# Masks, PSUM banks, the end of the experts and the rows handed to the mixers

## The chip, the cores and the metric

The kernel runs on one core of a Trainium2 chip. The metric is the device time of one execution in microseconds (us); a comparison takes the median of several runs. Engines are named as the profile names them: PE (TensorE, matmuls), PEld (its weight loads), DVE (VectorE), ACT (ScalarE), POOL (GpSimd) and SP (SyncE, which issues most DMAs). Each engine works through its own queue in order.

## The reference

Three blocks follow one another on 256 tokens of width 1024, in float32:

```python
def reference(x, c, ...):
    x = first_block(...)    # Fourier and conv branches, then a mixture of 16 experts, final norm
    x = second_block(...)   # "hybrid": compressed and windowed attention, block attention, gated merge, w_o
    return third_block(...) # two layers of four token mixers and a feed-forward, final norm

# first_block, experts: each expert takes its 32 best tokens
a = einsum('becd,edf->becf', xe, w_gate_e); u = einsum('becd,edf->becf', xe, w_up_e)
y = einsum('becf,efd->becd', silu(a) * u, w_down_e)
y = y * vals[..., None]                       # then added back at the tokens' rows
x = x + gate_f[:, None, :] * moe_out; return rms_norm(x, g_final)
# second_block, end
return x + rms_norm_2(m @ w_o, norm_post)
# third_block, one layer
h = rms_norm_3(x, attn_norm[l]); proj = h @ w_in[l]
o_a = neighborhood_attention(qa, ka, va, na_rpb[l])   # bias by offset, masked to 8 x 16 neighbours
o_b = diff_attention(qb, kb, vb, lam, ..., t5_diff)   # bias table t5, heads 0 to 3
o_c = dilated_attention(qc, kc, vc, t5_dil)           # bias table t5, heads 4 to 7, three windows merged
o_d = mla_attention(q_nope, q_rope, k_nope, k_rope, v_d)
x = x + concat([o_a, o_b, o_c, o_d]) @ w_o[l]
x = x + (silu(h2 @ w_gate[l]) * (h2 @ w_up[l])) @ w_down[l]
```

The dilated attention merges three windows; the kernel does it with one softmax whose scores get the t5 bias and a mask `c_dil`, the logarithm of how many of the windows hold the offset (and -1e30 where none does). Its value depends on the offset of key and query alone.

## The kernel before

**Storage and products.** Tokens lie in two halves (h = 0, 1) of 128 partitions, `x` is 128 x 2 x 1024. A projection needs the input transposed (features on partitions, tiles k = 0 to 7 of 128 features). To get float32 accuracy every operand is split into two fp32r parts, high and low (`hi`, `lo`; `wh`, `wl`): ACT casts the high part (L125 for weights, L284 for inputs), DVE subtracts for the low part (L126, L285), and PE makes three matmuls (L173, L174, L175) for each k and half. `proj` (L149) takes two PSUM banks, one for each half, and works through the weights in the order of their loads: k by k, for both halves. With `ahead=3` the last three pieces are split first and then run half by half, so that half 0 is evacuated while half 1 computes. Weights come through six ring slots, loaded by SP in an order fixed by `load` (L75).

**PSUM.** There are eight banks: pool `mm` has five (projections, attention scores, expert accumulators), `tr` two (transposes, L271), and `po` one. In `po` lie the up product of an expert (`psU`), the attention outputs (`po`), the output of the differential heads (`od`, L1603), one accumulator of `shift_scale`, the Fourier output and the router's `pb`.

**Queues.** The program is written in one order, and a scheduler of the framework orders the instructions of each engine by when they are ready in its model. Side work (generators, stepped by `pump` after each product piece) puts attention between projections. `tc.issue_after(ins)` keeps an instruction behind another. `N.held` (L130) keeps the next splits of weights behind an instruction.

**End of the experts** (L780 to L910). The last expert runs its down projection in two halves of 512 columns, each: 16 float32 matmuls L901 into `py` (the profile counts two records for each, so 32), `Y` = `py` times gate (L903, DVE), two matmuls that scatter `Y` to the tokens (`acc`, L907, four records), then `out(n)` (L813): two adds to `x`, transposes (L271) with their splits, squares, gain. Meanwhile the first weights of the hybrid block are loaded into ring slots and split there (`next_load`), and their products with the first input half's tiles k = 0 to 3 (`next_products`, 24 matmuls) are put into the second half after the fourth of its 16 matmuls; tiles 4 to 7 come at the end.

**Hybrid block to mixers** (L1245 to L1293). `w_o_2` runs in two chunks of 512 columns; the evacuation of the last (L1280 to L1287) makes the norm and adds `mo` times `r` to `x`, half by half in four steps of 256 columns. Then `nxt.half(c)` transposes four feature tiles of both halves at once, 128 x 256 for a split. The mixers' first projection, 416 columns (`chunk(2304, 416, ...)`, L1491), reads that input from the tile `hx`, which until then held the operand `mh`, `ml` of `w_o_2`.

**Mixers** (L1319 on, once in each of two layers). The projections run with four attention groups beside them: MLA first (its softmax reads the scores straight from the bank: L1395, ACT L1404), then differential, neighbourhood and dilated heads. `bias_rows` (L1296) in block 1 computes the t5 table for all offsets into DRAM (`t5d`); `na_bias` loads a 128 x 2048 tile and adds a mask to it on POOL (L1366); `dil_bias` loads the t5 tile, loads `c_dil` into an `m2` slot (L1372), and adds it on POOL in four adds (L1374). `m2` is a pool of scratch tiles: four in block 1, eight in the mixers.

## Time and profile before

| what | us |
|---|---|
| median of 3 runs | 2061.4 (2057.15 to 2067.67) |
| profiled execution | 2060.89 |
| its span, first to last instruction | 2059.1 |
| PE busy | 1658.0 (81%) |
| DVE busy | 810.1 (39%) |
| ACT busy | 602.7 (29%) |
| POOL busy | 171.9 (8%) |
| chain that ended last | PE 47%, DMA 43%, DVE 6%, issue 2% |

The span has stages: block 1 to about 252 us, the experts to about 1154, their end to 1190, the hybrid block to 1395, the way into the mixers to 1430, mixers and feed-forward of layer 0 to 1745, and of layer 1 to the end. A row of a timeline gives start, duration, engine, line, operation, output <- input, the count, and in brackets how long the engine was idle before it and what released it. A window gives each engine's busy time and instruction count, the mean granted clock of PE (1.00 is 2.4 GHz, 0.50 is 1.2 GHz), the busy share of the DMA engines and their GB/s.

### The profile page before, as it was taken

The numbers are of one execution on the slowest core, as the hardware profiler recorded it, in microseconds if no ns is written. First come the engines' busy times: TensorE is split into PE (matmuls) and PEld (weight loads), VectorE is DVE, ScalarE is ACT, GpSimd is POOL, SyncE is SP. The second block draws the span as 40 slices with busy tenths as digits, with TensorE's granted clock in tenths as the row PEclk, the third lists the DMA queues.
The fourth block names the chain that finished last, engine by engine and source line by source line (L and its number), as shares of the span: only waits on it lengthen the run. The fifth ranks groups of instructions, "written<-read, shape, count | busy, mean of one in ns | idle before, by whom it ended". The sixth has DMA issues, their size and how long they took to land.

```text
span 2059.1 us, 22375 instructions
## 1 busy us (share of the span) xinstructions
PE 1658.0 (81%) x8897; PEld 997.9 (48%) x8897; DVE 810.1 (39%) x1565; ACT 602.7 (29%) x1075; POOL 171.9 (8%) x135
## 2 busy tenths in 40 slices
PE   7999796665655565656555799999999999999998
PEld 4777631111111111111111387777768888768886
DVE  4788610000000000000000357786885555785554
ACT  4455410000000000000000245555554445555443
POOL 1652100000000000000000131102000000110000
PEclk9999898768788888887887999999999999999999
DMA  9988789999999999999999873446335556525552
GB/s 361 378 297 340 319 363 429 429 428 429 430 428 430 429 428 431 429 430 429 429 428 430 332 257 127 143 136 221 117 103 184 184 172 218 170 68 184 184 174 72
DMA packets 128441, 616.24 MB, mean 299 GB/s; under 512 B 8264, under 2 KB 17672, under 8 KB 101328
## 3 DMA queue, kind: packets, MB, share of 16 engines
q1 hardware_dynamic: 124336, 601.46, 74.1%
q0 software_dynamic: 3568, 12.75, 1.9%
q8 instruction: 70, 1.15, 0.2%
q10 hardware_dynamic: 432, 0.60, 0.1%
q14 instruction: 35, 0.29, 0.0%
HBM read 613.72 MB, written 4.24 MB: 300 GB/s over the span
## 4 chain that ended last, share of the span: by engine, by line
PE 47%; DMA 43%; DVE 6%; issue 2%; ACT 1%; SPq 1%; POOL 0%; POOLq 0%; ACTq 0%; DVEq 0%
DMA wr<-we_gate_dram 13%; DMA wr<-we_up_dram 13%; DMA wr<-we_down_dram 13%; PE pb L173 13%; PE pb L174 12%; PE pb L175 12%; DMA wr<-w_in_dram 2%; DVE wl L126 2%; PE pb L271 1%; DMA wr<-w_ada_dram 1%; PE pb L851 1%; PE pb L1413 1%; PE pb L901 1%; ACT sb L1404 1%; PE pb L793 1%
## 5 line engine op out<-in xcount | busy, mean ns | idle before, releaser
L126 DVE TENSOR_TENSOR wl<-wr,wh 128x1024 fp32r<-128x1024 f32 (+1 forms) x380 | 410.2, 1088 | 263.5 <-ACT wh L125 260.0
L851 PE MATMUL pb<-wr,XT 128*32 128x512 f32 x2048 | 319.4, 753 | 214.7 <-DMA wr<-we_up_dram 121.6
L125 ACT CAST wh<-wr 128x1024 fp32r<-128x1024 f32 (+1 forms) x380 | 339.9, 898 | 329.8 <-PE pb L175 302.3
L173 PE MATMUL pb<-wh,hx 128*128 128x512 f32 (+3 forms) x992 | 388.5, 392 | 3.4 <-ACT sb L1404 2.0
L174 PE MATMUL pb<-wl,hx 128*128 128x512 f32 (+3 forms) x992 | 376.6, 380 | 1.7 <-DVE wl L126 1.6
L175 PE MATMUL pb<-wh,hx 128*128 128x512 f32 (+3 forms) x992 | 377.2, 381 | 0.0
L851 PEld LDWEIGHTS pb<-wr,XT 128*32 128x32 f32 x2048 | 61.3, 124 | 454.5 <-DMA wr<-we_up_dram 198.4
L901 PE MATMUL pb<-wr,hT 128*32 128x512 f32 x1024 | 172.7, 803 | 103.0 <-DMA wr<-we_down_dram 96.4
L868 DVE TENSOR_TENSOR hs<-pb,hs 128x512 f32<-128x512 f32 x16 | 11.1, 691 | 554.9 <-PE pb L851 554.9
L173 PEld LDWEIGHTS pb<-wh,hx 128*128 128x128 f32 x992 | 187.2, 189 | 44.0 <-issue 5.8
L174 PEld LDWEIGHTS pb<-wl,hx 128*128 128x128 f32 x992 | 187.7, 189 | 36.5 <-DVE wl L126 4.5
L175 PEld LDWEIGHTS pb<-wh,hx 128*128 128x128 f32 x992 | 187.4, 189 | 35.4 <-issue 0.7
L867 ACT ACTIVATE hs<-pb 128x512 f32<-128x512 f32 x16 | 9.6, 598 | 535.3 <-PE pb L851 534.2
L901 PEld LDWEIGHTS pb<-wr,hT 128*32 128x32 f32 x1024 | 33.9, 129 | 221.0 <-DMA wr<-we_down_dram 143.2
L903 DVE TENSOR_TENSOR Y<-pb,gfr 128x512 f32<-128x512 f32 x15 | 10.4, 692 | 247.1 <-PE pb L901 247.1
L881 ACT COPY Sc<-pb 128x256 f32<-128x256 f32 x16 | 6.0, 373 | 310.3 <-PE pb L879 310.3
L821 POOL TENSOR_TENSOR x<-x,grow 128x512 f32<-128x512 f32 x4 | 5.6, 1420 | 890.5 <-ACT jk L260 890.5
L173 PE MATMUL pb<-wh,ah 128*128 128x512 f32 x176 | 69.9, 397 | 0.0
L174 PE MATMUL pb<-wl,ah 128*128 128x512 f32 x176 | 69.6, 395 | 0.0
L175 PE MATMUL pb<-wh,al 128*128 128x512 f32 x176 | 69.6, 395 | 0.0
L907 PE MATMUL acc<-Y,Sc 64*128 64x512 f32 (+1 forms) x128 | 40.7, 714 | 18.3 <-DVE Y L903 18.3
L404 POOL TENSOR_SCALAR wr<-wr,cs 128x768 f32<-128x768 f32 x14 | 40.3, 2878 | 31.3 <-DMA wr<-w_ada_dram 26.4
(504 smaller groups left out, 1727.4 us busy)
## 6 DMA issues: line engine op xcount, KB each, us to landing
wr<-we_gate_dram SPq DMA_DIRECT2D x64, 2048.0 KB, 38.9
wr<-we_up_dram SPq DMA_DIRECT2D x64, 2048.0 KB, 39.0
wr<-we_down_dram SPq DMA_DIRECT2D x63, 2048.0 KB, 38.9
wr<-w_in_dram SPq DMA_DIRECT2D x62, 1024.0 KB, 8.0
wr<-w_ada_dram SPq DMA_DIRECT2D x24, 1024.0 KB, 12.7
wr<-w_gate_dram SPq DMA_DIRECT2D x22, 1024.0 KB, 5.1
wr<-w_up_dram SPq DMA_DIRECT2D x22, 1024.0 KB, 5.0
wr<-w_down_dram SPq DMA_DIRECT2D x20, 1024.0 KB, 5.0
```

The lines of the kernel that those rows point to most:

```text
L125: self.nc.scalar.copy(hi, src)
L126: self.nc.vector.tensor_tensor(lo, src, hi.bitcast(F32), ALU.subtract)
L173: nc.tensor.matmul(o, xh[:, kt, tok], hv[:, k, :], start=kt == first, stop=False)
L174: nc.tensor.matmul(o, xh[:, kt, tok], lv[:, k, :], start=False, stop=False)
L175: self.last_mm = nc.tensor.matmul(o, xl[:, kt, tok], hv[:, k, :], start=False, stop=kt == last).ins
L271: self.nc.tensor.transpose(pv[:, j, h * P:(h + 1) * P], src[:, h, (k + j) * P:(k + j + 1) * P], self.ident)
L404: nc.gpsimd.tensor_scalar(wp, wp, cs[:, k:k + 1], None, ALU.mult)
L793: nc.tensor.matmul(pg, part[:, h, k * P:(k + 1) * P], G[:, h, es].rearrange("p e c -> p (e c)"), start=(h == 0 and i == 0), stop=(h == 1 a ...
L851: N.last_mm = nc.tensor.matmul(pacc[32 * j:32 * j + 32, :], XT[:, k + kk, e, :], wt[:, kk, j * 512:(j + 1) * 512], start=(k + kk == 0), st ...
L901: nc.tensor.matmul(py[32 * q:32 * q + 32, :], hT[:, b, 32 * j:32 * j + 32], wt[:, i, n * 512 - c0:n * 512 - c0 + 512], start=first, stop=l ...
L907: nc.tensor.matmul(acc[n][h], Sc[r, h * P:(h + 1) * P], Y[r, :], start=(e == 0), stop=(e == NE - 1))
L1404: nc.scalar.activation(sb[:, c], (ps if bias is None else sb)[:, c], AF.Exp, bias=mm[:, h:h + 1], accum_out=sm[:, h:h + 1])
```

## The change

The edits, in the order of the file:

- **PSUM.** The pool `po` is gone and `mm` has six banks; all that lay in `po` comes from `mm`.
- **A head in proj.** `lead=n` splits the first n pieces, then runs their products for half 0 and after that for half 1. The mixers' first projection of layer 0 uses `lead=3`.
- **Rows by halves.** `InputT.rows(h)` transposes one token half: two banks of four 128 x 128 transposes, each tile split by itself. The hybrid block queues `rows(0)` right behind half 0's adds and calls `rows(1)` at the end, then the squares. `mh`, `ml` move from `hx` to two tiles of the pool `ap82`. `N.held` keeps one split behind the second step of half 0's adds, where before three stood behind that of half 1.
- **End of the experts.** `out` issues the next load, and its splits only behind the second add of `x`. The second half's matmuls L901 and the products are chained in written order: eight of the sixteen L901 (`at + i`), the products of tiles 0 and 1, the other eight, tile 2 behind `Y`, tile 3 behind the adds, tiles 4 to 7 at the end.
- **Masks.** `c_dil` becomes an 8 x 512 table over heads and offsets (zero for heads 0 to 3). `bias_rows` loads it into the tile `t5sb` and adds the product to it, where before it copied the product; `dil_bias` with its load and four adds is gone. The mask of `na_bias` is added in eight operations of 128 x 256, where before it was one of 128 x 2048.

```diff
-        self.mm, self.tr, self.po = ps("mm", 5), ps("tr", 2), ps("po", 1)
+        self.mm, self.tr = ps("mm", 6), ps("tr", 2)
...
+        if lead:
+            head = [(k, piece, self.split_w(piece)) for k, piece in islice(pieces, lead)]
+            for h in range(2):
+                for k, piece, hl in head:
+                    self.proj_piece(ps, xh, xl, k, piece, n, hl=hl, hs=(h,))
...
+    def rows(self, h):
+        N, nc, tok = self.N, self.N.nc, slice(h * P, (h + 1) * P)
+        for k in range(0, KT, 4):
+            pv = N.bank(N.tr).rearrange("p (k t) -> p k t", t=P)
+            for j in range(4):
+                nc.tensor.transpose(pv[:, j, :], N.x[:, h, (k + j) * P:(k + j + 1) * P], N.ident)
+            for j in range(4):
+                g = self.gain[:, k + j:k + j + 1]
+                nc.scalar.activation(self.hi[:, k + j, tok], pv[:, j, :], AF.Copy, scale=g)
+                nc.vector.scalar_tensor_tensor(self.lo[:, k + j, tok], pv[:, j, :], g, self.hi[:, k + j, tok].bitcast(F32),
+                                               ALU.mult, ALU.subtract)
...
-            if n:
-                with tc.issue_after(add):
-                    next_load()
+            ahead = next_load()
+            next(ahead)
+            with tc.issue_after(add):
+                next(ahead, None)
+            if n:
+                next_products(1)
...
-                        if c0 and at + i == 4:
-                            next_products()
+                        if c0 and at + i == 8:
+                            next_products(2)
...
+                            with N.queued() if c0 else nullcontext():
+                                mm = nc.tensor.matmul(py[32 * q:32 * q + 32, :], ...
+                            if c0:
+                                N.last_mm = mm.ins
                 nc.vector.tensor_tensor(Y, py, ...)
+                if c0:
+                    next_products(1)
...
-                    self.po = N.po.tile([P, 512], F32, tag="b", name="po")
+                    self.po = N.bank(N.mm, "po")
...
-        mh, ml = N.hT()
+        mh, ml = N.T("mh"), N.T("ml")
...
-                        if q == 256 and h == 1:
-                            N.behind(st.ins)
+                        if q == 256 and h == 0:
+                            N.held = [st.ins]
+                    if h == 0:
+                        N.soon(lambda: nxt.rows(0))
...
+        nxt.rows(1)
         for c in range(2):
-            nxt.half(c)
+            nxt.squares(c)
...
-    nc.vector.tensor_copy(sb, pb[:8, :])
+    nc.gpsimd.dma_start(sb, a["c_dil"])
+    nc.vector.tensor_tensor(sb, pb[:8, :], sb, ALU.add)
...
-            nv = nb.rearrange("p h n (r c) -> p (h n r) c", c=64)
-            nc.gpsimd.tensor_tensor(nv, nv, nmask.unsqueeze(1).to_broadcast([P, 32, 64]), ALU.add)
+            for h in range(2):
+                for n in range(4):
+                    nv = nb[:, h, n, :].rearrange("p (r c) -> p r c", c=64)
+                    nc.gpsimd.tensor_tensor(nv, nv, nmask.unsqueeze(1).to_broadcast([P, 4, 64]), ALU.add)
...
-        def dil_bias():
-            td = t5_bias(4, "t5b")
-            dm = N.m2.tile([P, 2, S], F32, tag="m2", name="dm")
-            nc.gpsimd.dma_start(dm, a["c_dil"].rearrange("p (h k) -> p h k", h=2))
-            for n in range(4):
-                nc.gpsimd.tensor_tensor(td[:, n], td[:, n], dm, ALU.add)
-            return td
...
-        chunk(2304, 416, [(crow, f1)])
+        chunk(2304, 416, [(crow, f1)], lead=0 if l else 3)
...
-                    od.append(N.bank(N.po))
+                    od.append(N.bank(N.mm))
```

## Rows read from the trace of the kernel before

**Rows 1.** Windows of the span by stage; the first line names the columns

```profile
core 0: us, PE busy (x) PEld busy (x) DVE busy (x) ACT busy (x) POOL busy (x), PEclk, DMA share, GB/s
252.00:1154.00 902.00, 552.36 (x3328) 130.59 (x3328) 52.13 (x102) 21.74 (x43) 3.18 (x3) 0.81 0.99 423
1154.00:1190.00 36.00, 29.40 (x149) 19.18 (x150) 20.47 (x38) 17.46 (x36) 11.71 (x16) 0.95 0.79 289
1395.00:1430.00 35.00, 31.54 (x142) 25.48 (x141) 25.59 (x68) 22.43 (x47) 6.30 (x10) 0.95 0.67 217
1430.00:1535.00 105.00, 100.02 (x546) 75.82 (x545) 80.45 (x230) 53.56 (x130) 15.30 (x12) 0.98 0.37 118
1760.00:1860.00 100.00, 93.32 (x516) 70.19 (x515) 79.56 (x219) 50.26 (x125) 11.29 (x8) 1.00 0.36 115
```

**Rows 2.** Timeline of DVE, end of the experts: start, duration, instruction, [idle before <- releaser]

```profile
1155.46 1.23 DVE L126 TENSOR_TENSOR wr<-wr 128x1024 fp32r<-128x1024 f32 x1 [9.53 <-ACT wr L125]
```

**Rows 3.** Timeline of PE, end of the experts

```profile
1157.43 3.45 PE L907 MATMUL acc<-Y,Sc 128*128 128x512 f32 x4 [3.96 <-DVE Y L903]
...
1162.48 1.06 PE L901 MATMUL pb<-wr,hT 128*32 128x512 f32 x8
...
1169.14 2.78 PE L901 MATMUL pb<-wr,hT 128*32 128x512 f32 x24
1172.74 1.98 PE L907 MATMUL acc<-Y,Sc 128*128 128x512 f32 x4 [0.81 <-DVE Y L903]
```

**Rows 4.** Issues of the last three loads of down weights: count, first and last start, landing

```profile
L75 SPq DMA_DIRECT2D wr<-we_down_dram x3: 4185/4212/4763, 1125.4 to 1133.9; - x3
...
DMA to landing us min/median/max: 30.0/31.9/33.7
```

**Rows 5.** Timeline of DVE, hybrid block to mixers

```profile
1395.01 1.67 DVE L1287 SCALAR_TENSOR_TENSOR x<-mo,ro_r,x 128x256 f32<-128x256 f32 x4 [0.70 <-POOL ro_r L241]
...
1399.07 1.67 DVE L1287 SCALAR_TENSOR_TENSOR x<-mo,ro_r,x 128x256 f32<-128x256 f32 x4 [0.67 <-POOL ro_r L241]
```

**Rows 6.** Timeline of PE, hybrid block to mixers

```profile
1396.24 0.39 PE L175 MATMUL pb<-wh,hx 128*128 128x512 f32 x1
...
1399.61 1.54 PE L271 MATMUL pb<-ident,x 128*128 128x128 f32 x6 [2.76 <-DVE x L1287]
```

**Rows 7.** Windows behind that wait and in the first mixers (columns as in rows 1)

```profile
1399.30:1402.40 3.10, 2.74 (x9) 2.30 (x10) 3.10 (x8) 2.27 (x7) 0.62 (x1) 0.51 0.00 0
1450.60:1454.00 3.40, 3.40 (x13) 2.93 (x12) 2.63 (x5) 1.23 (x2) 0.00 (x0) 0.50 0.00 0
```

**Rows 8.** Timeline of PE, mixers of both layers, its waits

```profile
1449.69 0.70 PE L1413 MATMUL pb<-qkT 96*128 96x256 f32 x2 [1.88 <-ACT sb L1404]
...
1772.60 0.50 PE L173 MATMUL pb<-wh,hx 128*128 128x512 f32 x1 [2.02 <-ACT sb L1404]
...
1776.38 0.70 PE L1413 MATMUL pb<-qkT 96*128 96x256 f32 x2 [1.66 <-ACT sb L1404]
```

**Rows 9.** Timeline of DVE, mixers of both layers, beside the mask's add

```profile
1441.61 2.78 DVE L126 TENSOR_TENSOR wl<-wr,wh 128x1024 fp32r<-128x1024 f32 x1
...
1766.23 5.12 DVE L126 TENSOR_TENSOR wl<-wr,wh 128x1024 fp32r<-128x1024 f32 x1
```

**Rows 10.** One line each: counts, least, median, longest ns, first and last start

```profile
L1366 POOL TENSOR_TENSOR nb<-nb,nmask x2: 4585/4711/4837, 1438.5 to 1765.7; 128x2048 f32<-128x2048 f32 x2
...
L1374 POOL TENSOR_TENSOR t5b<-t5b,dm x8: 1262/1296/1320, 1490.6 to 1819.4; 128x512 f32<-128x512 f32 x8
...
L1420 DVE TENSOR_SCALAR sb<-sb,cs x64: 338/349/1355, 1445.8 to 1849.7; 128x256 f32<-128x256 f32 x64
```

**Rows 11.** Waits of SP's queue, 118 to 140 us

```profile
SPq L75 <- DVE modT L390: 12.1, 1, 12.1
```

**Rows 12.** Window of block 1 (columns as in rows 1)

```profile
138.00:169.10 31.10, 31.10 (x137) 25.44 (x137) 25.00 (x29) 16.46 (x27) 18.22 (x8) 0.97 0.86 319
```

**Rows 13.** Timeline of POOL, block 1

```profile
192.05 0.59 POOL L1310 DMA_DIRECT2D t5v<-t5sb  x1 [23.00 <-DVE t5sb L1309]
```

More of the change, by code (lines that the diff above doesn't have):

```diff
@@ L2 @@
 from contextlib import ExitStack, contextmanager, nullcontext
+from itertools import islice
 import numpy as np
@@ L147, in split_w, with proj @@
         return hv, lv
-    def proj(self, xh, xl, loads, n, evac, ahead=0):
+    def proj(self, xh, xl, loads, n, evac, ahead=0, lead=0):
         ps = [self.bank(self.mm), self.bank(self.mm)]
@@ L1448, in st3 @@
                     return
-                po = N.po.tile([P, 512], F32, tag="b", name="po")
+                po = N.bank(N.mm, "po")
                 pts = [pTs.pop(n - 1), pTs.pop(n)]
@@ L1785, in consts @@
     c["c_t5oh"] = (np.arange(32)[:, None] == bucket[None, :]).astype(np.float32)
[L1787 to L1788 removed]
+    mult = sum(((o % dil == 0) & (np.abs(o) <= w // 2)).astype(np.int64) for w, dil in ((128, 1), (512, 4), (2048, 16)))
     lm = np.where(mult > 0, np.log(np.maximum(mult, 1)), -1e30)
[L1790 removed]
+    c["c_dil"] = np.arange(8)[:, None] // 4 * lm[None, :]
     col = np.arange(64)
```

42 lines of the change are left out of this document (21 added, 21 removed).

## The prediction

> **What bounds the kernel now.** I read the windows by stage first [rows 1]. In the experts (252 to 1154 us) the DMA share is 0.99, so 902 us of the span belong to the loads; a bank, a mask or an order on PE is worth nothing there. The other stages are bound by PE, whose idle time is small: the end of the experts is busy for 29.40 of 36.00 us, the way into the mixers for 31.54 of 35.00, the mixers for 100.02 of 105.00 in layer 0 and 93.32 of 100.00 in layer 1. That is 6.6 + 3.5 + 5.0 + 6.7 = 21.8 us of idle PE, and all that the change can win lies in it and in matmuls that run long because the granted clock is low after a wait. Then the timelines of these four places, for which wait ends last [rows 2, 3, 5, 6, 8], the windows for the clock behind a wait [rows 7], and the lines of DVE and POOL that hold the late step [rows 9, 10]. The reader is to see that the late step is mostly not PE's own: DVE stands in its queue behind a split that waits for something else, or behind POOL.
>
> **End of the experts.** Before, DVE waits 9.53 us for the cast of a loaded weight, and the gate product Y, queued behind that split, lets PE wait 3.96 us at 1157.43 although its last L901 was done at 1153.47 [rows 2, 3]. The following acc matmuls take 3.45 us where the same four take 1.98 at 1172.74 [rows 3]: 1.5 us lost to the clock. So of this stage 6.6 + 1.5 = 8.1 us are loss. The change puts the splits behind the add to x. Y then follows at once: behind the second half the step from the last L901 to acc costs 0.81 [rows 3], so acc starts near 1154.3, 3.1 earlier. The second order is in PE's queue: before, 24 products (from 1163.54 to 1169.14, 0.233 each) stood in front of the last 24 records of L901 [rows 3]. Their weights had landed: the three loads were issued from 1125.4 to 1133.9 and took 33.7 to 30.0 us, so the first lay there at 1159.1 and the last at 1163.9 [rows 4]. After, 16 records, 12 products, 16 records: up to 1163.9 PE has the acc (2.0 to 3.5), transposes (under 2), about 24 records (2.8) and the 12 products (2.8), some 10 us of work in the 10.4 since 1153.47. The last 8 records take 1.06 [rows 3], so the second Y could start at 1165.0 and its acc at 1165.8, with the product of tile 2 (6 x 0.233) beside it 1166.4, in place of 1172.74: 6.3 us, the upper end. It isn't all gain, since up to 12 of the products, 2.8 us, move behind that acc, where they fill gaps or not. What is late next is DVE: first the add to x, then splits of 1.23 each [rows 2], then tile 0's products, which now stand in front of the second 16 records in a fixed order. If the first acc runs at the low clock the adds end near 1159, the splits at 1161.7, the products at 1164.5, the records (24 took 2.78) at 1166.4, acc at 1167.2. I keep 3 of the 8.1 us as loss (two waits for Y, the adds, the landing) and take **5 us**, between 2 and 6.5. No load is removed, and the hybrid block behind it starts that much earlier.
>
> **Hybrid block to mixers.** The last matmul of w_o_2 starts at 1396.24, then PE waits 2.76 us for half 1's adds on DVE [rows 6], and in the next 3.10 us the clock is 0.51 [rows 7], worth 1.5: 4.3 us in all, the upper end with little room over it. After, half 0's adds are done at 1396.7 (1395.01 + 1.67 [rows 5]), so eight transposes and the head's nine products of half 0 can lie in the wait; half 1's adds start at 1399.07 [rows 5] in either order, since the norm sets them. But DVE is the limit: it is busy for 3.10 of 3.10 us behind the wait [rows 7], and now it has to split the first weights before, and 16 input splits of half the size in place of 8. If these cost in proportion to their size, nothing is added; if half of a split is fixed cost, about 1.5 us. And whether the head's products stand in front of half 1's transposes is for the scheduler: in the written order they stand behind them, and then the wait is filled by the transposes of half 0 alone. From -0.5 to 4, I take **2 us**, near the middle, because DVE's queue stays full. The splits held behind the adds are one in place of three, which helps DVE's order rather than PE's. The new home of mh and ml takes two of four tiles of that pool; the tile that mo needs then is the one of the merge, read for the last time before w_o_2 begins: 0.
>
> **Mixers: masks.** POOL's add of the neighbourhood mask runs 4.84 us at 1438.5 and 4.59 at 1765.7 [rows 10]; a weight split of 128 x 1024, 1.23 alone [rows 2], takes 2.78 and 5.12 beside it [rows 9]: 1.55 and 3.89 us more, and ends when the add ends. Behind the split on DVE stands the step of the MLA softmax on which ACT's exponential waits, and PE waits for that: 2.02 at 1772.60 [rows 8]. With eight adds of about 4.7 / 8 = 0.6 us (0.65 by half of the 1.30 for 512 columns [rows 10]) the split waits for one of them at most if it gets in between. The four adds of c_dil cost POOL 4 x 1.30 a layer [rows 10]; beside them DVE's scaling L1420 took up to 1.355 us where its median is 0.349 [rows 10], about 2 us of DVE a layer for a pair. They go entirely, and the load that waited for a scratch slot too. Here the rule of the Trainium skill, "SBUF — State Buffer", section "Who interferes with whom", speaks against half of this: a DVE instruction with two SBUF inputs and a GpSimd one that reads SBUF exclude each other for a whole instruction, so eight short adds block in turns where one long one blocked once. The rows agree with an exclusion (the split ended with the add); that the turns are bounded is the forecast. By the rule each of the splits in the stretch may pay 0.65.
>
> **Mixers: banks.** Three waits of PE in the MLA heads are for a bank that ACT reads: 1.88, 2.02 and 1.66 us [rows 8], 5.56 together, and in layer 0 the clock stays at 0.50 for 3.40 us after [rows 7], 1.7 more: 7.3. A sixth bank lets PE go one step further ahead, but outputs and the differential heads' od now lie in the six, and od is held over some heads; while both are held the pool is as small as before. From -1 (od in the way) to 7.3. With the masks' share (up to 1.8 more through DVE) I take **5 us** for both layers' mixers, range 0 to 9: the waits hang on the same DVE and ACT steps, and what PE does earlier it may wait for later.
>
> **Block 1 and the rest.** One more load of 0.59 on POOL, which there idles for 23.00 us [rows 13], and an add in place of a copy on DVE. In the experts both products now share a pool with py; the loads set that stage: 0, between -1 and +1.
>
> **The sum.** 5 + 2 + 5 = 12 us. 2060.9 - 12 = 2048.9, and the profiled execution stands 0.5 below the median of 2061.4, so I forecast **2049**.
>
> **Rivals.**
> Only the experts' end pays. The junction and the mixers stay bound by DVE and ACT: for it speak DVE at 3.10 of 3.10 [rows 7] and at 80.45 of 105.00 and 79.56 of 100.00 in the mixers [rows 1]; against it, that the two long splits are plainly POOL's doing [rows 9]. It includes that the change doesn't do what it says, the head's products standing behind half 1's transposes. 2061 - 5 = 2056.
> Everything pays: 6.5 + 3.5 + 9 = 19, so 2042. Against it: the 21.8 us of idle time would nearly all have to go.
> The exclusion works in turns: splits and other two-input steps on DVE pay for short adds one by one, so that 3.5 of the mixers' 5 remain: 2050.5. For it, that a DVE step of 0.35 grew to 1.355 beside adds of 1.30 [rows 10]. It is where the rule named above (the Trainium skill, "SBUF — State Buffer", section "Who interferes with whom") points; these rows agree with it as far as they go.
> Slower: the load of c_dil sits in POOL's queue in block 1 and waits for a scratch slot. There are four; SP already waited 12.1 us for one [rows 11], and c_dil's tile comes after it and the two tables' tiles. Behind it on POOL stand the multiplications of w_ada, 18.22 us of work between 138.0 and 169.1 [rows 12], which keep ring slots that SP loads into. If the load is queued at 138 and its slot comes late, at the latest before 192.05, where the tile is written out [rows 13], this work ends up to 192 + 18 = 210 and not at 169, and up to 41 us of loads are put off; the experts start so much later. I take 30, since a slot comes back before its new tile is done with. It decides as soon as more is lost than the 12 won: 2049 + 30 = 2079. Against it: POOL's idle time before 192.05 [rows 13] is a place where the load would fit, behind that work.
>
> **How the numbers follow.** The bound that a measurement here can tell from no change is 0.5%, 10.3 us: faster means under 2051.1, slower over 2071.7. Chances: forecast 0.42 (2044 to 2054), only the experts' end 0.27 (2053 to 2060), everything 0.13 (2037 to 2044), turns 0.10 (2048 to 2053), slower 0.08 (2065 to 2080). Faster: 0.13, about 0.35 of the forecast's, 0.06 of the turns and 0.01 of the second, 0.55. Slower: 0.08, and 0.09 with what isn't thought of; 0.36 are left for the same. For the range I leave out the slower case and a part of the largest gain: 2040 to 2060. The terms' own bounds (2 to 6.5, -0.5 to 4, 0 to 9, -1 to 1) give from 0.5 to 20.5 us, the same range within a microsecond.
>
> **What would show it.** Right: acc of the first half starts near 1154.3 and that of the second near 1167; PE's wait of 2.76 is under 1 and the clock behind it 1.00; both splits beside the mask's adds under 2 us, no PE wait over 1 us in the MLA heads, the load of c_dil in POOL's idle stretch. Wrong: an add or a split on DVE standing behind a cast again at the experts' end; PE waiting for a bank whose reader is od; a new wait of equal size a few microseconds behind each of the old ones; or the experts' first loads starting later than before.

## The result: 2042.8 us, 0.93% faster

The changed kernel takes 2042.78 us (median of 4 runs, 2040.85 to 2045.02) where before takes 2062.47 (4 runs in the same comparison, 2057.15 to 2067.67): a ratio of 0.9907, interval 0.9883 to 0.9932, or 19 us less, between 14 and 24. The profiled execution took 2043.8 us with a span of 2042.0, against 2060.89 and 2059.1. The forecast was 2049 with a range of 2040 to 2060, so the sign and the range held; the gain was 17 to 19 us and not 12, and it did not come from where the sum had put it.

To see where, each operation of DVE, ACT and PE was paired with the same one in before (the n-th of a kind with the n-th, where both have as many), and the median of the differences in start taken over stretches. That needs no guess at where a stage begins. Steps between two columns are what a stage gave. There is one profile of each kernel, and how far a step can be trusted is to be read from kernels with the same code at a place: `x_pools` and `x_best` are alike up to the last expert and stand 3.9 and 1.1 us ahead there, so the first column is known to some 3 us. Without an edit at the end of the experts its step is -0.6 to +0.6 (`m_split`, `m_fold`, `j_rows`), and without one on the way into the mixers -0.1 to +0.6. The dilated bias and the tails agree to 0.2.

| kernel | up to the last expert | end of experts | hybrid block | into the mixers | MLA heads, layer 0 | dilated bias, 0 | tail, 0 | MLA, layer 1 | dilated, 1 | tail, 1 | at the end |
|---|---|---|---|---|---|---|---|---|---|---|---|
| forecast | 0 | -5 | 0 | -2 | -5 for both layers' mixers | | | | | | -12 |
| after | -2.9 | -4.3 | +1.4 | +0.5 | -2.3 | -2.0 | -1.3 | -3.0 | -2.0 | -1.3 | -17.1 |
| m_fold | -4.4 | +0.2 | 0.0 | +0.6 | +1.1 | -2.0 | 0.0 | -2.4 | -2.0 | 0.0 | -8.7 |
| m_split | -1.3 | -0.6 | 0.0 | 0.0 | -2.4 | +0.1 | 0.0 | -3.7 | 0.0 | 0.0 | -7.6 |
| p_banks | -2.2 | +1.3 | +1.1 | +0.2 | +3.1 | 0.0 | -1.4 | -2.3 | +0.2 | -1.4 | -0.8 |
| d_end | -1.2 | -6.2 | 0.0 | +0.3 | +1.1 | +0.2 | 0.0 | -0.2 | +0.1 | 0.0 | -5.5 |
| e_splits | -1.5 | -3.3 | 0.0 | -0.1 | +2.8 | 0.0 | 0.0 | 0.0 | 0.0 | 0.0 | -2.0 |
| j_rows | -0.6 | +0.6 | +0.2 | +0.4 | +0.9 | +0.1 | 0.0 | -2.4 | +0.1 | 0.0 | -0.4 |
| a_cols | -1.8 | -4.6 | +1.1 | +0.4 | -2.6 | -2.0 | -1.4 | -3.9 | -2.0 | -1.5 | -17.9 |
| a_nolead | -3.7 | -5.0 | +1.4 | +0.5 | -2.4 | -2.0 | -1.3 | -3.0 | -2.0 | -1.3 | -18.7 |
| a_po | -1.7 | -4.3 | +0.2 | +0.3 | -2.5 | -2.0 | 0.0 | -3.1 | -2.0 | 0.0 | -14.6 |
| a_two | -3.0 | -4.2 | +1.3 | +0.6 | 0.0 | -1.9 | -1.3 | -3.8 | -2.0 | -1.3 | -15.5 |
| x_pools | -3.9 | -5.7 | +0.2 | +0.4 | -2.7 | -2.0 | -1.4 | -2.9 | -2.0 | -1.4 | -20.8 |
| x_best | -1.1 | -4.6 | +0.2 | +0.2 | -2.4 | -2.0 | -1.4 | -3.0 | -2.0 | -1.4 | -17.3 |

(Differences in us against the profile of before; small steps in the feed-forward stretches, up to 0.7, are left out, so the columns don't add up exactly. The kernels are those of the experiments below.)

The windows of the changed kernel that hold the same work as the end of the experts and the mixers in [rows 1], columns as there:

```profile
1151.90:1182.80 30.90, 28.97 (x149) 19.29 (x150) 19.89 (x38) 16.56 (x36) 11.69 (x16) 0.94 0.88 321
1424.70:1524.20 99.50, 96.48 (x545) 73.30 (x545) 77.51 (x230) 52.99 (x130) 12.43 (x14) 1.00 0.37 122
1749.30:1843.00 93.70, 91.19 (x516) 69.41 (x515) 74.22 (x220) 49.90 (x125) 7.71 (x10) 1.00 0.38 119
```

The stage of 36.00 us is now 30.90 with 28.97 of PE, that of 105.00 is 99.50, and that of 100.00 is 93.70. PE's idle time in the three has gone from 6.6, 5.0 and 6.7 us to 1.9, 3.0 and 2.5.

**End of the experts.** DVE, then PE, to be read against [rows 2, 3]:

```profile
1151.40 0.69 DVE L933 TENSOR_TENSOR Y<-pb,gfl 128x512 f32<-128x512 f32 x1 [7.21 <-PE pb L928]
...
1156.53 2.35 DVE L127 TENSOR_TENSOR wr<-wr 128x1024 fp32r<-128x1024 f32 x2
```

```profile
1152.23 3.65 PE L939 MATMUL acc<-Y,Sc 128*128 128x512 f32 x4 [0.88 <-ACT wr L126]
...
1157.48 1.92 PE L928 MATMUL pb<-wr,hT 128*32 128x512 f32 x16
...
1162.27 1.92 PE L928 MATMUL pb<-wr,hT 128*32 128x512 f32 x16
...
1165.64 1.88 PE L939 MATMUL acc<-Y,Sc 128*128 128x512 f32 x4
```

Y (L933) no longer stands behind a split: the splits (L127) come after it, behind the adds. The first acc waits 0.88 us where it waited 3.96, and the second half runs as 16 records, 12 products, 16 records, with tile 2's product beside Y. Its acc starts at 1165.64, 7.1 us earlier than before, of which 2.9 were there ahead of this stage. The first acc still takes 3.65 us, at a mean granted clock of 0.53 (1152.2 to 1155.9), after PE had waited 2.02 us for a down weight at 1148.24. That isn't the edit's doing: with the same edit it takes 1.95 us in `d_end`, at a clock of 1.00, and 3.75 in `a_two`.

**Mixers.** The split beside the mask's adds, in layer 0 and 1, the second four adds of layer 0, and the lines of the two operations (compare [rows 9, 10]):

```profile
1436.31 1.70 DVE L127 TENSOR_TENSOR wl<-wr,wh 128x1024 fp32r<-128x1024 f32 x1
...
1755.49 1.29 DVE L127 TENSOR_TENSOR wl<-wr,wh 128x1024 fp32r<-128x1024 f32 x1
...
1436.20 3.79 POOL L1405 TENSOR_TENSOR nb<-nb,nmask 128x256 f32<-128x256 f32 x4 [1.34 <-DMA nb<-rpbd]
```

```profile
L1405 POOL TENSOR_TENSOR nb<-nb,nmask x16: 717/730/1781, 1430.3 to 1758.0; 128x256 f32<-128x256 f32 x16
...
L1451 DVE TENSOR_SCALAR sb<-sb,cs x64: 341/348/552, 1440.0 to 1832.6; 128x256 f32<-128x256 f32 x64
```

The split takes 1.70 and 1.29 us where it took 2.78 and 5.12; the scaling of the scores (L1451, before L1420) at most 0.552 where it was 1.355. The waits of [rows 8] are gone; what is left in their place is one for a bank of transposes, 1.2 us in layer 0 and 0.8 in layer 1:

```profile
PE pb L277 <- ACT rows L1505: 1.2, 1, 1.2
```

### The profile page after: what moved, and what is told of

The parts are those of the page before. It is cut to its first block, busy times and chain, and to the rows that moved or that the text cites. A ratio compares the mean times of both kernels' runs of the same rounds, so it can differ in the third digit from the quotient of the medians.

```text
span 2042.0 us, 22402 instructions
## 1 busy us (share of the span) xinstructions
PE 1655.3 (81%) x8897; PEld 994.9 (49%) x8897; DVE 802.5 (39%) x1573; ACT 601.6 (29%) x1083; POOL 164.8 (8%) x140
## 4 chain that ended last, share of the span: by engine, by line
PE 48%; DMA 43%; DVE 5%; issue 2%; ACT 1%; SPq 1%; POOL 0%; POOLq 0%; ACTq 0%; DVEq 0%
DMA wr<-we_gate_dram 13%; DMA wr<-we_up_dram 13%; PE pb L179 13%; DMA wr<-we_down_dram 13%; PE pb L180 13%; PE pb L181 13%; DMA wr<-w_in_dram 2%; DVE wl L127 2%; PE pb L277 1%; SPq L76 1%; PE pb L879 1%; PE pb L928 1%; DMA wr<-w_ada_dram 1%; PE pb L1444 1%; ACT sb L1435 1%
## 5 line engine op out<-in xcount | busy, mean ns | idle before, releaser
L127 DVE TENSOR_TENSOR wl<-wr,wh 128x1024 fp32r<-128x1024 f32 (+1 forms) x380 | 405.6, 1076 | 260.7 <-ACT wh L126 257.4
L179 PE MATMUL pb<-wh,hx 128*128 128x512 f32 (+3 forms) x960 | 376.0, 392 | 3.1 <-ACT wh L126 2.0
L180 PE MATMUL pb<-wl,hx 128*128 128x512 f32 (+3 forms) x960 | 363.3, 378 | 1.8 <-DVE wl L127 1.8
L181 PE MATMUL pb<-wh,hx 128*128 128x512 f32 (+3 forms) x960 | 364.1, 379 | 0.2 <-DVE hx L339 0.2
L179 PEld LDWEIGHTS pb<-wh,hx 128*128 128x128 f32 x960 | 180.8, 189 | 41.8 <-ACT wh L126 5.0
L180 PEld LDWEIGHTS pb<-wl,hx 128*128 128x128 f32 x960 | 181.2, 189 | 35.1 <-DVE wl L127 4.4
L181 PEld LDWEIGHTS pb<-wh,hx 128*128 128x128 f32 x960 | 180.9, 188 | 35.3 <-DVE hx L339 0.8
L933 DVE TENSOR_TENSOR Y<-pb,gfr 128x512 f32<-128x512 f32 x15 | 10.4, 691 | 244.1 <-PE pb L928 244.1
```

Source lines behind the costliest of these rows:

```text
L127: self.nc.vector.tensor_tensor(lo, src, hi.bitcast(F32), ALU.subtract)
L179: nc.tensor.matmul(o, xh[:, kt, tok], hv[:, k, :], start=kt == first, stop=False)
L180: nc.tensor.matmul(o, xh[:, kt, tok], lv[:, k, :], start=False, stop=False)
L181: self.last_mm = nc.tensor.matmul(o, xl[:, kt, tok], hv[:, k, :], start=False, stop=kt == last).ins
```

## The experiments

### m_fold: the mask of the dilated heads alone

```diff
-    nc.vector.tensor_copy(sb, pb[:8, :])
+    nc.gpsimd.dma_start(sb, a["c_dil"])
+    nc.vector.tensor_tensor(sb, pb[:8, :], sb, ALU.add)
...
-        td = dil_bias()
+        td = t5_bias(4, "t5b")
```

> Before with c_dil folded into the t5 table alone (no load of it and no four adds in the mixers). Theory A (each part of the change pays by itself where its late step was): the stretch from 1490 to 1500 us of layer 0 and its like in layer 1 lose 2.0 us each, as in the kernel after, and the MLA stretch and the tail of the mixers stay as before: -4 us in all, and about -1 in block 1 from what is released earlier there. Rival B (the gain of that stretch is the sixth bank's): the stretch stays, DVE's scaling L1420 is short but PE waits on a bank in its place: 0 to -1 us.

Measured: 2054.52 us against 2061.10, ratio 0.9971 (0.9959 to 0.9982). The two stretches lose 2.0 us each, as theory A has it and as in all kernels with this edit, so rival B falls; the longest scaling of the scores takes 0.355 us here. The 1 us that theory A sees in block 1 is there too: between 170 and 195 us all eight kernels with this edit gain 1.1 us, and the five without it none (0 to 0.3 lost). Not expected: the MLA heads changed too, by +1.1 in layer 0 and -2.4 in layer 1, without an edit there. The split of weights beside the mask's add, in layer 0 and then in layer 1, each with POOL's add behind it:

```profile
1438.14 5.49 DVE L126 TENSOR_TENSOR wl<-wr,wh 128x1024 fp32r<-128x1024 f32 x1
...
1437.98 4.57 POOL L1367 TENSOR_TENSOR nb<-nb,nmask 128x2048 f32<-128x2048 f32 x1 [4.95 <-DMA nb<-rpbd]
...
1761.88 2.77 DVE L126 TENSOR_TENSOR wl<-wr,wh 128x1024 fp32r<-128x1024 f32 x1
...
1758.14 5.41 POOL L1367 TENSOR_TENSOR nb<-nb,nmask 128x2048 f32<-128x2048 f32 x1 [1.78 <-issue]
```

In layer 0 the add starts at 1437.98, 0.16 us ahead of the split, which takes 5.49 us; in layer 1 it has run for 3.7 us when the split starts, and the split takes 2.77. In both the split ends 1.08 to 1.10 us after the add does (1437.98 + 4.57 and 1438.14 + 5.49; 1758.14 + 5.41 and 1761.88 + 2.77), as it does in [rows 9] with the add at 1438.46 (4.84 us, so to 1443.30; the split to 1444.39). DVE does the split's work only when the add is over.

### m_split: the mask of the neighbourhood heads alone

```diff
-            nv = nb.rearrange("p h n (r c) -> p (h n r) c", c=64)
-            nc.gpsimd.tensor_tensor(nv, nv, nmask.unsqueeze(1).to_broadcast([P, 32, 64]), ALU.add)
+            for h in range(2):
+                for n in range(4):
+                    nv = nb[:, h, n, :].rearrange("p (r c) -> p r c", c=64)
+                    nc.gpsimd.tensor_tensor(nv, nv, nmask.unsqueeze(1).to_broadcast([P, 4, 64]), ALU.add)
```

> Before with the neighbourhood mask's add in eight operations alone. Theory A: the split of 128x1024 beside it takes under 2 us in both layers, the MLA stretch is 2.2 us shorter in layer 0 and 3.0 in layer 1, as in the kernel after: -5 us. Rival B (banks carry that stretch): the split is shorter but the waits of PE for a bank that ACT reads stay, since ACT is late by its own work: -1 us at most. Rival C (exclusion in turns): the split of 128x1024 still takes 2 us or more in layer 0, and layer 1 alone gains, -2 us.

Measured: 2055.93 us, ratio 0.9974 (0.9963 to 0.9985). The MLA heads are 2.4 and 3.7 us shorter: theory A, and with no sixth bank. DVE's split and POOL's adds, four before it and four around it:

```profile
1439.78 1.33 DVE L126 TENSOR_TENSOR wl<-wr,wh 128x1024 fp32r<-128x1024 f32 x1
...
1433.56 2.81 POOL L1369 TENSOR_TENSOR nb<-nb,nmask 128x256 f32<-128x256 f32 x4 [0.15 <-issue]
...
1439.30 3.78 POOL L1369 TENSOR_TENSOR nb<-nb,nmask 128x256 f32<-128x256 f32 x4 [2.19 <-DMA nb<-rpbd]
```

The split takes 1.33 us and POOL pays: the four adds beside it take 3.78 where the four before took 2.81. So the two do take turns, as rival C has it, but the turn that DVE waits for here is the rest of one short add.

### a_two: the mask in two adds, for the length of a turn

```diff
-            for h in range(2):
-                for n in range(4):
-                    nv = nb[:, h, n, :].rearrange("p (r c) -> p r c", c=64)
-                    nc.gpsimd.tensor_tensor(nv, nv, nmask.unsqueeze(1).to_broadcast([P, 4, 64]), ALU.add)
+            for h in range(2):
+                nv = nb[:, h].rearrange("p n (r c) -> p (n r) c", c=64)
+                nc.gpsimd.tensor_tensor(nv, nv, nmask.unsqueeze(1).to_broadcast([P, 16, 64]), ALU.add)
```

> The changed kernel with the neighbourhood mask's add in two operations of 128x1024. Theory A (DVE's weight split waits for the one add of POOL that is under way, so what it loses is at most an add's length, and how much is set by where it meets it): an add takes 2.3 to 2.5 us, the split beside it takes between 1.23 and 3.7, and the MLA stretch of each layer lies between the changed kernel's and 2.4 (layer 0) or 3 us (layer 1) more. Rival (what counts is only that the first half of the bias is masked earlier): same times as the changed kernel, splits of 1.3 to 1.7 us.

Measured: 2045.38 us (one run). In layer 0 the split meets an add that has just begun:

```profile
1436.25 3.15 DVE L127 TENSOR_TENSOR wl<-wr,wh 128x1024 fp32r<-128x1024 f32 x1
...
1435.92 2.39 POOL L1404 TENSOR_TENSOR nb<-nb,nmask 128x1024 f32<-128x1024 f32 x1 [2.75 <-DMA nb<-rpbd]
```

It takes 3.15 us, again to 1.09 after the add's end (1438.31), and the gain of the MLA heads there is gone (0.0 in the table); in layer 1 the same kernel's split meets none, takes 1.32, and the gain is 3.8. That is theory A: the length of the add under way, and where it is met.

### p_banks: six banks alone

```diff
-        self.mm, self.tr, self.po = ps("mm", 5), ps("tr", 2), ps("po", 1)
+        self.mm, self.tr = ps("mm", 6), ps("tr", 2)
...
-                    self.po = N.po.tile([P, 512], F32, tag="b", name="po")
+                    self.po = N.bank(N.mm, "po")
```

(and the other uses of `po` likewise)

> Before with po merged into mm (six banks) alone. Theory A: the tail of the mixers (1510 to 1530 us and its like) is 1.3 us shorter in each layer, the last heads of the hybrid block 1.4 longer (as in the kernel after, where PE waits for pT at 1351 and 1353), the MLA stretch unchanged, block 1 about 1 shorter: -2 us. Rival B: the MLA stretch is 2.2 and 3.0 shorter with this edit alone: -7 us.

Measured: 2065.19 us, ratio 1.0017 (1.0008 to 1.0027): slower, against theory A's -2. Of its ten runs seven took 2065.1 to 2067.0 us and three 2059.9 to 2062.0. The profiled one is among the three (2060.06), so the trace shows where 0.8 us were won and not where the other seven lost 4 to 6. In it theory A has the places right (tails -1.4 and -1.4, hybrid block +1.1), and the MLA heads change after all, by +3.1 in layer 0 and -2.3 in layer 1. In layer 0 the split beside the mask is long (DVE's split, then POOL's add, which began 0.26 us ahead of it):

```profile
1441.95 5.41 DVE L126 TENSOR_TENSOR wl<-wr,wh 128x1024 fp32r<-128x1024 f32 x1
...
1441.69 4.59 POOL L1366 TENSOR_TENSOR nb<-nb,nmask 128x2048 f32<-128x2048 f32 x1 [4.67 <-DMA nb<-rpbd]
```

How the long add meets DVE explains layer 1: the split beside it takes 2.77 or 2.78 us in `p_banks`, `m_fold` and `j_rows`, and the heads gain 2.3 to 2.4; it takes 4.99 and 5.10 in `d_end` and `e_splits`, near the 5.12 of [rows 9], and they gain 0.2 and nothing. In layer 0 the split's length isn't all: 5.49 in `m_fold` and 5.54 in `d_end` go with +1.1, the 5.41 here with +3.1. And in `e_splits` (+2.8) and `j_rows` (+0.9) the split was done before, and the long step is a tiny one of the softmax itself, 0.15 us elsewhere, with one input, on which ACT's exponential waits. In `e_splits`, where POOL's add runs from 1437.55 for 4.71 us:

```profile
1437.78 4.53 DVE L1405 TENSOR_SCALAR cm<-cm 128x2 f32<-128x2 f32 x1
```

Rival B isn't borne out: layer 0 got longer, and `m_split` has the gain with five banks. The waits of [rows 8] were for a bank in name, but the bank came late because a step of DVE held up the softmax. The hybrid block's loss is two waits that before doesn't have:

```profile
PE po L1141 <- DVE pT L1128: 1.1, 2, 0.8
```

### a_po: the changed kernel without the merged pool

```diff
-        self.mm, self.tr = ps("mm", 6), ps("tr", 2)
+        self.mm, self.tr, self.po = ps("mm", 5), ps("tr", 2), ps("po", 1)
```

> The changed kernel with the two pools of before (mm with five banks, po with one). Theory A (banks: 1.4 us won in each tail of the mixers, 1.4 lost in the hybrid block's last heads, about 1 lost at the experts' end, 0 in the MLA heads once the masks are short): within 1 us of the changed kernel. Rival B (the sixth bank carries the MLA stretch, 2 to 3 us a layer): 5 to 6 us slower than the changed kernel.

Measured: 2044.45 us against 2060.88, ratio 0.9917 (0.9900 to 0.9934), 1.7 us above the changed kernel's median and within the intervals of both. The table has theory A's tails, hybrid block and MLA heads: both tails lose their 1.3, the hybrid block regains 1.2, and the heads are as short as with six banks, so rival B falls. The loss of 1 us that it put at the experts' end isn't there (-4.3 in both kernels). What the sixth bank does in a tail is to be seen on the scores of the last pair of dilated heads, which take two banks: before, then the changed kernel, then this one:

```profile
1515.36 1.13 PE L1413 MATMUL pb<-dl 64*128 64x256 f32 x4
...
1519.38 1.13 PE L1413 MATMUL pb<-dl 64*128 64x256 f32 x4
```

```profile
1505.84 0.70 PE L1444 MATMUL pb<-dl 64*128 64x256 f32 x4
...
1507.06 0.70 PE L1444 MATMUL pb<-dl 64*128 64x256 f32 x4
```

```profile
1505.43 1.13 PE L1444 MATMUL pb<-dl 64*128 64x256 f32 x4
...
1509.45 1.13 PE L1444 MATMUL pb<-dl 64*128 64x256 f32 x4
```

The two chunks of w_o hold four banks there. With one bank left the pair's second four records start 4.0 us after its first four (1519.38 and 1515.36; here 1509.45 and 1505.43), with two 1.2 us after (1507.06 and 1505.84), and four take 0.70 in place of 1.13.

This kernel also has the exception to `m_split`. In layer 1 a split starts 0.42 us before the first of four short adds and ends 1.09 us after the last of them (1753.22 + 2.81 and 1752.80 + 4.32); it did not get in between:

```profile
1752.80 4.32 DVE L127 TENSOR_TENSOR wl<-wr,wh 128x1024 fp32r<-128x1024 f32 x1 [3.17 <-ACT wh L126]
...
1753.22 2.81 POOL L1405 TENSOR_TENSOR nb<-nb,nmask 128x256 f32<-128x256 f32 x4
```

The MLA heads of that layer are 3.1 us shorter all the same, and PE's longest wait there is 0.9 us. But that a split waits for one short add at most is not so.

### d_end and e_splits: the end of the experts, whole and half

`d_end` is before with all edits of that stage. `e_splits` is before with the load and the splits of `out` alone:

```diff
-            if n:
-                with tc.issue_after(add):
-                    next_load()
+            ahead = next_load()
+            next(ahead)
+            with tc.issue_after(add):
+                next(ahead, None)
```

> Before with the new end of the experts alone. Theory A: from the last matmul L901 of the first half to the dense products of the hybrid block 5.1 us less, as in the kernel after, and no other stage changes: -5 us. Rival: without the sixth bank the second half's matmuls have to wait for the bank that Y reads, and the two banks of the products for the adds, so that 2 us remain: -2 us.

> Before with the end of the experts changed in its load and splits alone (splits behind the add to x in both halves); the products of tiles 0 to 3 stand in the second half after its fourth matmul and are not chained, as before. Theory A (two edits, half each): acc of the first half starts 3.1 us earlier, near 0.9 us after the last L901, and the second half's acc 2 to 3 us earlier than before, against 6 with both edits: the hybrid block starts 3 us earlier. Rival (it is all Y's place behind the split): 5 to 6 us as with both edits.

Measured: `d_end` 2053.91 us against 2061.10, ratio 0.9968 (0.9959 to 0.9978), and 6.2 us less in its stage, so the sixth bank isn't needed (theory A); the seven kernels that hold this edit with the rest gain 4.2 to 5.7 there. `e_splits` 2058.93 (one run) against 2061.41, and 3.3 us less in the stage: theory A there too. PE's rows of `e_splits`, then of `d_end`:

```profile
1152.86 1.96 PE L911 MATMUL acc<-Y,Sc 128*128 128x512 f32 x4 [0.91 <-DVE Y L907]
...
1164.29 2.78 PE L905 MATMUL pb<-wr,hT 128*32 128x512 f32 x24
1167.89 1.98 PE L911 MATMUL acc<-Y,Sc 128*128 128x512 f32 x4 [0.81 <-DVE Y L907]
```

```profile
1152.52 1.95 PE L920 MATMUL acc<-Y,Sc 128*128 128x512 f32 x4 [0.91 <-DVE Y L914]
...
1157.32 1.92 PE L909 MATMUL pb<-wr,hT 128*32 128x512 f32 x16 [1.19 <-DMA wr<-we_down_dram]
...
1162.12 1.92 PE L909 MATMUL pb<-wr,hT 128*32 128x512 f32 x16
...
1165.49 1.88 PE L920 MATMUL acc<-Y,Sc 128*128 128x512 f32 x4
```

With the splits moved alone, the first acc waits 0.91 us and runs at a granted clock of 1.00 (1.96 us), and the second half's 24 records stand behind the 24 products still, at 1164.29. With the chained order they run at 1157.32 and 1162.12, and the second acc follows the first after 12.97 us in place of 15.03. Both halves of the edit count: 3.3 us for the splits, the rest of 6.2 for the order.

### j_rows, a_cols and a_nolead: rows by halves and the head

`j_rows` is before with that part alone; `a_cols` is the changed kernel without it; `a_nolead` only without the head:

```diff
-        chunk(2304, 416, [(crow, f1)], lead=0 if l else 3)
+        chunk(2304, 416, [(crow, f1)])
```

> Before with the rows by halves and the head alone. Theory A: the way into the mixers is as long as before to within 0.5 us; what changes in the mixers behind it is only how the long mask add meets the weight split (up to 2 us either way): -1 to +2 us. Rival B: the way into the mixers is 2 us shorter, and the time -2 us.

> The changed kernel without the rows by halves and the head (transposes of both halves at once, mh and ml in hx, three splits held, as before). Theory A (the junction's gain was eaten: new short waits in place of the one long one, 0.5 us worse by the offsets): within 1 us of the changed kernel, the stretch from the last product of w_o_2 to the end of the first projection about 0.5 shorter. Rival B (the rows by halves did bring their 2 us, and the merged banks lost them in the hybrid block): 2 us slower than the changed kernel.

> The changed kernel with rows by halves, but without the head of three k tiles half by half. Theory A (the head is what lets half 0's products run before half 1's transposes): PE waits 2 to 2.5 us for half 1's adds again, and the clock falls behind it, so 2 to 3 us slower than the changed kernel up to the first mixers' projection. Rival: the small splits on DVE and ACT set the pace and the head is worth nothing: within 0.5 us of it.

Measured: `j_rows` 2060.59 against 2060.88, ratio 1.0000 (0.9991 to 1.0010). `a_cols` 2042.63, ratio 0.9908 (0.9893 to 0.9923), the same as the changed kernel. `a_nolead` 2043.25, ratio 0.9912 (0.9897 to 0.9927). So this part gives nothing, with or without the rest: theory A's times for the first two. (That the stretch from the last product of w_o_2 to the end of the first projection is 0.5 shorter without it is not so: 16.35 us in `a_cols`, 14.73 in the changed kernel, where the transposes of half 0 stand ahead of that product.) For the third theory A is wrong: without the head PE's waits are those of the changed kernel to the tenth, and the mixers' first product starts at 1391.12, ahead of half 1's adds at 1396.07, all the same. The waits of PE on the way into the mixers, of the changed kernel (`a_nolead` has the same two) and of `a_cols`, the longest each:

```profile
PE pb L179 <- ACT hx L338: 1.1, 3, 0.5
PE pb L335 <- DVE x L1319: 0.5, 1, 0.5
```

```profile
PE pb L277 <- DVE x L1319: 2.8, 1, 2.8
```

The one wait of 2.8 us is gone with the edit, and from half 0's first add to the last matmul of the first projection it is nevertheless longer: 17.8 us (1389.41 to 1407.21) against 17.2 before (1395.01 to 1412.19). It is 17.8 in all seven kernels with the rows by halves, and 17.0 to 17.6 in the seven without them. The windows of this stretch, before and after:

```profile
1395.00:1412.20 17.20, 14.26 (x72) 12.76 (x71) 13.88 (x31) 11.82 (x25) 6.30 (x10) 0.90 0.48 158
```

```profile
1389.40:1407.20 17.80, 15.45 (x71) 11.21 (x71) 14.36 (x39) 12.42 (x32) 6.31 (x10) 1.00 0.44 146
```

DVE is busy for 13.88 of 17.20 and for 14.36 of 17.80 us. Its order in the changed kernel:

```profile
1393.91 0.68 DVE L1312 TENSOR_TENSOR mo<-pb,prow 128x512 f32<-128x512 f32 x1
...
1395.27 0.15 DVE L1315 TENSOR_TENSOR sso<-sso 128x1 f32<-128x1 f32 x1
...
1395.40 1.01 DVE L127 TENSOR_TENSOR wl<-wr,wh 128x832 fp32r<-128x832 f32 x1
1396.33 0.60 DVE L339 SCALAR_TENSOR_TENSOR hx<-pb,vecs,hx 128x128 fp32r<-128x128 f32 x2
1396.85 0.14 DVE L244 TENSOR_SCALAR ro_t<-sso 128x1 f32<-128x1 f32 x1
1397.67 1.67 DVE L1319 SCALAR_TENSOR_TENSOR x<-mo,ro_r,x 128x256 f32<-128x256 f32 x4 [0.68 <-POOL ro_r L247]
```

Half 1's norm goes mo (1393.91), sum of squares (1395.27), its scaled mean (1396.85), POOL's root, adds (1397.67). Between these small steps stand now splits of half 0 (L339) and of the weights (L127, 1.01 us). The adds start 5.2 us behind the last matmul of w_o_2 (1392.48), where they started 2.8 behind it [rows 5, 6]. And that matmul itself is later: it starts 3.07 us after half 0's adds where it was 1.23, since half 0's transposes and a wait of 0.53 us for those adds now stand in front of it. So half 1's adds follow half 0's after 8.26 us in place of 4.06, 4.2 later: 2.4 by DVE's order, 1.8 by PE's.

### x_pools and x_best: pools by stage, and the norm first

`x_pools` is the changed kernel with five banks and one up to the end of the hybrid block and six from there; `x_best` holds in addition two of the head's splits behind half 1's norm:

```diff
         inp = block2(N, stop)
+        N.banks.close()
+        N.mm = ctx.enter_context(tc.tile_pool(name="mm6", bufs=6, space=bass.MemoryType.PSUM))
```

```diff
                     if h == 0:
                         N.soon(lambda: nxt.rows(0))
+                    else:
+                        N.held = [N.last_rstd] * 2 + N.held
```

> The changed kernel with five banks and one (mm, po) up to the end of the hybrid block, and six from the mixers on. Theory A: the hybrid block's last heads regain the 1.1 us that the merged pool cost there, the tails of the mixers keep their 1.3 each: 1 us faster than the changed kernel. Rival (the hybrid block's loss is the rows by halves): as the changed kernel.

> The kernel with the pools by stage, and the second and third split of the head held behind the norm of half 1 (its reciprocal root on POOL), so that DVE does that norm's steps before them. Theory A (half 1's adds came 2.3 us later behind w_o_2 than before, since splits stood in front of the norm's small steps on DVE): the adds come 1 to 2 us earlier, the way into the mixers is 1 to 2 us shorter than in the changed kernel, 2 to 3 us in all. Rival (the small input splits on ACT and DVE set the end of the first projection): the adds come earlier, the end of the first projection doesn't: 1 us in all, from the pools.

Measured: `x_pools` 2042.76 against 2061.41, ratio 0.9907 (0.9891 to 0.9924); `x_best` 2042.64, ratio 0.9905 (0.9890 to 0.9920). By the table the pools by stage do regain the hybrid block's 1.2 us (+0.2 in place of +1.4), but the time of the whole doesn't show it: its median is the changed kernel's, and 1 us is less than the interval of either. The holding did not do what it was to do: DVE's order is as before, a weight split at 1395.74 ahead of the scaled mean at 1397.19,

```profile
1395.74 1.01 DVE L129 TENSOR_TENSOR wl<-wr,wh 128x832 fp32r<-128x832 f32 x1
...
1397.19 0.14 DVE L246 TENSOR_SCALAR ro_t<-sso 128x1 f32<-128x1 f32 x1
```

and half 1's adds start 5.18 us behind the last matmul of w_o_2, as in `x_pools` and the changed kernel. So theory A and its rival for `x_best` are not told apart; an order with the norm first wasn't had. One thing speaks for the rival: with the pools by stage, in `x_pools` and `x_best` alike, PE waits there for a bank that mo reads,

```profile
PE pb L181 <- DVE mo L1314: 1.8, 1, 1.8
```

1.8 us more than in the changed kernel, and the first projection ends as there all the same (last w_o_2 matmul to its last matmul: 14.71 us in both, 14.73 in the changed kernel). With DVE's order unchanged, 1.8 us of PE didn't matter.

## Why the forecast was right, and where it wasn't

**Right: the end of the experts.** Forecast 5 us (2 to 6.5); it gave 4.3 in the changed kernel and 6.2 alone. The mechanism is the one told, and the two edits share it. What spreads the gain is in part the clock of the first acc, 3.65 or 1.95 us, which the prediction had as a case of its own.

**Wrong in size and in cause: the mixers.** Forecast 5 us, bounds 0 to 9; measured 11.8 (5.5 in layer 0, 6.3 in layer 1), above the upper bound. Three terms:
- The MLA heads gave 2.3 and 3.0. The step "a sixth bank lets PE go one step further ahead" put the 7.3 us of [rows 7, 8] to the banks. `m_split` gives 2.4 and 3.7 with the old banks, and `a_po` has 2.5 and 3.1 with them; so the sixth bank did not carry it. The wait named a bank, but the late step was DVE's split, 1.55 and 3.89 us too long, which the prediction had priced beside it as "up to 1.8 more", without a working for the 1.8.
- The dilated mask gave 2.0 in each layer, 3.9 together. The step that found "about 2 us of DVE a layer" was right (the rows of before have 1.12 and 1.35 for a pair, so 1.8); the sum then didn't carry it.
- The tails gave 1.3 in each layer, and no sentence of the prediction speaks of them. There the sixth bank is worth something, because four are held by w_o.

**Wrong: hybrid block to mixers.** Forecast 2 us (-0.5 to 4); measured -0.5 in the profile, which kernels without the edit there show too (up to +0.6 in the table), and `j_rows` shows the part worth nothing. The step that failed is "half 1's adds start at 1399.07 in either order, since the norm sets them". The norm's steps on DVE are short but many, and work for half 0 was put between them, so that the adds came 2.4 us later behind w_o_2, and w_o_2's last products themselves 1.8 later behind half 0's adds. That an order with the norm first would have won the 2 us is not shown, since `x_best` didn't get one. The prediction's signs for this place came true (PE's longest wait is 0.5, the clock 1.00) and the time didn't: they were signs that PE's wait was filled, not that the stretch ended earlier. "DVE is the limit" was in the same paragraph, and would have given the right end of the range. That the head of `proj` wouldn't be needed was not foreseen: the scheduler had already put half 0's products ahead.

**Missed: the hybrid block.** Forecast 0 for it, measured +1.4, of which 1.1 to 1.2 are the merged pool (`p_banks`, `a_po`, `x_pools`).

**The rivals.** "Only the experts' end pays" is out. "Everything pays" has the time, 2042, by luck: its terms were 6.5, 3.5 and 9, and what came was 4.3, -0.5 and 11.8, with 2.9 ahead of the experts' end and 1.4 lost in the hybrid block. That the measured time lies inside the range owes something to luck too: the mixers' 11.8 lie above their bound, and the way into them and the hybrid block gave some back. "The exclusion works in turns" is what happens (`m_split`), but a turn of an eighth is cheap enough that it costs a few tenths; only in `a_po` did four turns pass in one. The scaling of the scores, with which that rival is argued, is not a two-input step: it reads one tile and a column of factors. The Trainium skill, "SBUF — State Buffer", section "Summary: rules for kernel authors", says that where DVE has two SBUF inputs and GpSimd's operation reads SBUF, the second to issue is blocked until the first is through; the runs agree: in six splits (two in before, two in `m_fold`, one each in `a_two` and `p_banks`) the end comes 1.08 to 1.10 us after the add's, however much of the add had passed when the split began. The split of `a_po` fits this less well, since by the profile it began ahead of the adds. The rival on the slower side did occur at its place: the load of c_dil stood in POOL's queue for 18.56 us, until a gate bias was read out, and a multiplication of w_ada stood behind it, at 179.71 where before the last one began at 164.77:

```profile
179.09 0.58 POOL L1344 DMA_DIRECT2D t5sb<-c_dil_dram  x1 [18.56 <-DVE gate L573]
179.71 2.36 POOL L423 TENSOR_SCALAR wr<-wr,cs 128x768 f32<-128x768 f32 x1
```

It cost nothing, since only one of the four pairs of multiplications was left behind it, and not all four as the price of 30 us had it; what these make, modT, was written at 204.7 us, before at 206.5. Of these 1.8 us 1.1 arise between 170 and 195 us, in every kernel with the folded mask (`m_fold`), so block 1, put at 0 between -1 and +1, won a little more than its bound. What in that stretch is shorter isn't shown. Against the price of 30 stood the row on POOL's idle time [rows 13]: the load's place was early in it, and the scheduler moved one pair to the other side.

**What stays open.** The changed kernel is 2.9 us ahead at the last expert. The folded mask brings 1.1 of it in block 1; whether the other 1.8 are the change's can't be told, since `x_pools` and `x_best`, alike up to there, differ by 2.8. By the ratios the parts won 6.0, 5.4 and 6.6 us (`m_fold`, `m_split`, `d_end`), lost 3.5 (`p_banks`) and 0 (`j_rows`), 14.5 together, and the whole 19. The difference may lie in the sixth bank, which lost 3.5 us with the long mask and gives the changed kernel some 2 (`a_po` 0.9917 against 0.9907, within the intervals of both). Why seven of ten runs of `p_banks` are 5 us or more above the profiled one is not shown; how the long mask meets DVE, which moves a layer by +3.1 to -2.4 us in `m_fold`, `d_end`, `e_splits`, `j_rows` and `p_banks`, is a candidate.

## What to carry to other kernels

A wait of PE for a bank says who reads the bank, not why the reader is late: follow that reader's queue back to the instruction that ran long, and price the edit there. A long operation on POOL beside a DVE step costs what is left of it when they meet, here also for a step of 128 x 2 with one input, and small shifts elsewhere move that meeting, so that a kernel with such an operation answers unrelated edits with gains and losses of several microseconds. Cut into eight it did so less: the heads gained 2.3 to 2.7 us in layer 0 and 2.9 to 3.9 in layer 1 in all seven kernels with the eight short adds. It is no bound, since a DVE step can miss every gap between them (`a_po`). Filling an engine's wait brings nothing where the filler's own steps stand, on another engine, in front of the steps that would have ended the wait.

## What the runs showed of the hardware

- A DVE subtraction of 128 x 1024 with both inputs in SBUF takes 1.23 us alone, and up to 5.54 (`d_end`, layer 0) beside one POOL addition of 4.6 us; it ends 1.1 us after the addition does. Beside four additions of 0.73 us it took 4.32 once (`a_po`, layer 1).
- A DVE step of 128 x 2 with one input takes 0.15 us alone and 4.5 beside the long addition (`e_splits` and `j_rows`, layer 0).
- DVE can hold up POOL too: of sixteen short additions with a median of 0.73 us one took 1.78.
- The eight short additions cost POOL 2.81 us for four undisturbed, so 5.6 for all where the long one takes 4.6 to 4.8 (5.0 to 5.4 where a split had begun just before it, in `m_fold` and `j_rows`): 0.7 us each for 256 columns against 1.3 for 512 and 2.4 for 1024.
- Four records of score matmuls over 64 rows take 1.13 us where one bank is at hand and 0.70 where two are.
